# A hybrid attention and state-space step: 16-bit halves put together by VectorE, squares from SBUF, and two transposes moved from TensorE to the DMA

## The chip, the cores and the metric

The kernel runs on one NeuronCore of a Trainium2 chip. The core has TensorE (PE in the profile; its weight loads are PEld), VectorE (DVE), ScalarE (ACT), GpSimd (POOL) and SyncE (SP, which here only issues DMAs). Each works through its own queue of instructions in order, and semaphores tie them together. SBUF is the working memory of 128 partitions, PSUM the memory that TensorE writes to, in banks of 512 fp32 columns; 16 DMA engines move data. The metric is the device time of one execution in microseconds (us), as the median of several runs.

## The reference, cut to what matters

One layer is computed for 1024 prompt tokens and 8 samples of 16 tokens, 1152 tokens in all, model width 1024:

```python
h = rms_norm(x, norm_g) * (1 + scale) + shift            # scale, shift, gate from c @ w_ada
proj = h @ w_in                                          # q k v z_att z_ssd xbc dt gates
q, k = rms_norm(q, q_norm_g), rms_norm(k, k_norm_g)      # 16 heads of 64
o_att = attn(q, k, v)        # own chunk of 64 and 8 before it, relative bias; samples: 512 cached rows and own
att_branch = (o_att * silu(z_att)) @ w_att_proj
xbc, conv_new = causal_dwconv(xbc, ...)                  # width 4
xs, bm, cm = split(silu(xbc))                            # 32 heads of 64; 4 groups of 128 states
# per chunk, a_cs = cumsum(dt * a):
xdt = xs * dt
y = ((cm @ bm.T) * decay) @ xdt + (cm @ h) * exp(a_cs)
h = h * exp(a_cs[-1]) + bm.T @ (xdt * exp(a_cs[-1] - a_cs))
y = rms_norm((y + d_skip * xs) * silu(z_ssd), ssd_norm_g)
merged = sigmoid(g_att) * att_branch + sigmoid(g_ssd) * (y @ w_ssd_proj)
out = x + gate * (merged @ w_out)
```

Outputs are `out` for both groups, the new keys and values, the convolution's last rows and the final states.

## The kernel before

All matmuls of a projection ("dense") take fp32 operands as a high and a low part, so three matmuls stand for one product (L459, L460, L462). The 1152 tokens stand in the columns, in three groups of 384. A projection of 128 output rows is 72 such matmuls. Its weights are loaded to `raw` (L329, on SP, two places), split by ScalarE (L351, high part) and VectorE (L352, low part).

The stages, in order:

- **Start**, to about 85 us: adaLN and the norm give h.
- **Attention**, eight rounds u of two heads. `dense_gen` computes q, k, v with tokens in the rows (`dense_tok`, L523 to L525, 24 matmuls for each of nine token tiles into a PSUM bank of the pool `psd`, which has two). `ev` empties the bank: L948 copies q and k to SBUF (ScalarE), L950 squares them out of PSUM (ScalarE), L951 copies v (VectorE), L954 sums the squares. Then follows the dense projection of the gate z of the next round. `prelude` normalizes q and k on POOL and turns them by TensorE (L1001). `prompt` computes scores in rounds (L1166), softmax (L1053 bias and minimum, L1048 exponential, L1049, L1050), and `turn` transposes the probabilities by DMA. A DMA transpose takes 16-bit elements, so the 32-bit words are first taken apart into a plane of high halves and one of low halves (L1097, `planes`, ScalarE), each plane is transposed in blocks of 128x128 (L1098, on SP), and the halves are put together again (`words`): for head e = 0 by VectorE (L1106), for e = 1 by ScalarE (L1104). `weigh` (L1122) multiplies by v.
- `sample` does the same for the samples, in two groups of four per round: scores (L1221, L1224), softmax, then `transposed`, five TensorE transposes (L1060) and their copies out of PSUM (L1062 ScalarE, L1064 VectorE), the product with the cached v (L1248), a copy (L1254) and the turn back (L1258).
- **State-space**, about 770 to 1550 us, 16 pairs p of heads in four groups. `dense_gen` of a pair projects x and z (and a gate for ten of the pairs), `conv_gen` does the convolution (L1306 to L1316, result x with channels in the rows). `prelude` makes the decay matrices `me` (L1487 loads, L1499, L1503, L1505). `main` turns x by nine TensorE transposes (L1527), of which VectorE takes two scaled copies out of PSUM (L1531): `xw` for the state, `xd` for the output. Then come small splits (L1553, L1554), masks on POOL (L1561), chunk states (L1572, L1577, L1581), the output (L1599, L1606), what the earlier states give (L1619, L1624, L1625), the gating (L1632), and the samples' states (L1644, L1653).
- **Tail**, from about 1550 us: the remaining gates and the three last projections.

What sets the order: the code is written as generators. `run` drives the dense projection and, beside it, the lists `urgent` and `paced`; a planner's clock counts what a step costs TensorE (`yield n`) and how long others are expected to take (`pause`, `until`). The places for buffers are planned too: `walloc` waits until one is free, and a dense projection may be two pairs ahead at most (`AHEAD`). Then the tile framework's scheduler orders each engine's instructions; those in `late` keep their order.

Of the kernel before, what the change touches and what calls it, by code (L numbers as in the profile page):

```python
# [9 lines left out]
U16 = mybir.dt.uint16  # L10
AF = mybir.ActivationFunctionType
ALU = mybir.AluOpType

P = 128
# [8 lines left out]
HD = 64  # L23
# [10 lines left out]
BIG = -1e30  # L34

# [87 lines left out]
def trunk_kernel(ctx: ExitStack, tc: tile.TileContext, h):  # L123
# [41 lines left out]
    def pg(cols=512):  # L165
        return psg.tile([P, 512], F32, tag="g", name=nm("g"))[:, :cols]
# [663 lines left out]
    def until(t):  # L830
        while clock[0] < t:
            yield -1.0

    def pause(t):
        yield from until(clock[0] + t)
# [77 lines left out]

    sfree = [0.0]
# [14 lines left out]
    def attention(u):  # L929
# [4 lines left out]
        def dense_gen():  # L934
# [7 lines left out]
            def ev(t, ps):  # L942
# [7 lines left out]
                nc.scalar.activation(s.ap, ps[:, :2 * P], AF.Square)  # L950
# [104 lines left out]
        def transposed(p, pt, nt):  # L1055
            for j in range(0, nt, 4):
                n = min(4, nt - j)
                ps = pg()
                for s in range(n):
                    nc.tensor.transpose(ps[:, s * P:(s + 1) * P], p[:, (j + s) * P:(j + s + 1) * P], ident)  # L1060
                if j == 0:
                    nc.scalar.activation(pt[:, j * P:(j + n) * P], ps[:, :n * P], AF.Copy)  # L1062
                else:
                    nc.vector.tensor_copy(pt[:, j * P:(j + n) * P], ps[:, :n * P])  # L1064

        def prompt():
# [8 lines left out]

            def planes(x, at, n):
                return x.ap[:, at:at + n * P].bitcast(U16).rearrange("p (t k) -> p t k", t=2)

            def words(x, at, n):
                return x.ap[:, at:at + n * P].bitcast(U16).rearrange("p (k t) -> p t k", t=2)  # L1080

            def turn(m):
# [11 lines left out]
                for e in range(2):  # L1094
                    yield from until(probs[m] + 800 * e)
                    (x, at), (y, _) = place[m][e], turned[m][e]
                    nc.scalar.activation(planes(y, at, n), words(x, at, n), AF.Copy)  # L1097
                    dma(x.ap[:, at:at + n * P].bitcast(U16).rearrange("p (i k) -> p i k", k=P),  # L1098
                        y.ap[:, at:at + n * P].bitcast(U16), transpose=True)
                for e in range(2):  # L1100
                    yield from until(probs[m] + 800 * e + 7500)
                    (x, at), (y, _) = place[m][e], turned[m][e]
                    if e:
                        nc.scalar.activation(words(y, at, n), planes(x, at, n), AF.Copy)  # L1104
                    else:
                        nc.vector.tensor_copy(words(y, at, n), planes(x, at, n))  # L1106
# [4 lines left out]
                tpt[m] = clock[0] + 4500  # L1111
# [86 lines left out]
        def sample():  # L1198
# [6 lines left out]
            for bg in range(2):  # L1205
# [34 lines left out]
                transposed(p.ap, pt.ap, 5)  # L1240
                p.free()
                yield 550
                yield from pause(1800)
# [202 lines left out]
    def ssd(p):  # L1446
# [62 lines left out]
        def main():  # L1509
# [11 lines left out]
            for j in range(3):  # L1521
                n = min(4, 9 - 4 * j)
                c = slice(4 * j * P, (4 * j + n) * P)
                ps = pg()
                for s in range(n):
                    t0 = (4 * j + s) * P
                    nc.tensor.transpose(ps[:, s * P:(s + 1) * P], x.ap[:, t0:t0 + P], ident)  # L1527
                v4 = lambda t: t.rearrange("p (c e d) -> p c e d", e=2, d=HD)
                for dst, sc in ((xw, w4), (xd, d4)):
                    f = sc[:, 4 * j:4 * j + n, 2 * p:2 * p + 2].unsqueeze(3).to_broadcast([P, n, 2, HD])  # L1530
                    nc.vector.tensor_tensor(v4(dst.ap[:, c]), v4(ps[:, :n * P]), f, ALU.mult)  # L1531
                yield 107 * n
# [438 lines left out]
```

## Time and profile before

| | |
|---|---|
| median of three runs | 1965.84 us (1962.32 to 1969.33) |
| the profiled execution | 1968.7 us, span 1966.9 us |
| PE busy | 1910.4 us, 97% |
| DVE, ACT, POOL busy | 1171.7, 902.4, 326.3 us |
| mean granted TensorE clock | 0.995 |
| queue q1 (SP's DMAs) | 239.22 MB, 42.0% of 16 engines |

A row of the grouped lines reads: line, engine, operation, output<-inputs, shapes, count, then busy us and mean ns of one, then the engine's idle time before them and what ended it. A row of waits reads: engine, line, what it waited for, us in total, times, longest. A row by stretch gives each engine's busy time with its number of instructions, then the granted TensorE clock, the DMA engines' share and GB/s. L-numbers are lines of the kernel before. Busy time of a pipelined PE is not PE at its peak, so stretches without a gap are read together with their count of matmuls.

### The profile page before, as it was taken

How to read it: one execution, taken by the hardware profiler on the slowest of the kernel's cores; microseconds unless marked ns; L12 is line 12 of the kernel's file. 1: busy time of each engine (PE TensorE's matmuls, PEld its weight loads, DVE VectorE, ACT ScalarE, POOL GpSimd, SP SyncE). 2: the span in 40 equal slices, each digit the busy share in tenths (PEclk: the TensorE clock that was granted, in tenths of full speed). 3: DMA queues.
4: the chain of work that ended last, by engine and by line, in shares of the span. 5: the costliest groups of instructions: out<-in, count | busy, mean ns of one | idle time of the engine just before them, and what ended most of it. 6: DMA issues, size and time to landing. Idle time of an engine off the chain costs nothing.

```text
span 1966.9 us, 34369 instructions
## 1 busy us (share of the span) xinstructions
PE 1910.4 (97%) x13561; PEld 1814.8 (92%) x13561; DVE 1171.7 (60%) x2411; ACT 902.4 (46%) x1653; POOL 326.3 (17%) x624
## 2 busy tenths in 40 slices
PE   8999998999989999999999999999999999999999
PEld 5988887887878789999999999999999999999999
DVE  7456555555555675667666666675675333777732
ACT  8466657566666777344444443436342301111210
POOL 0312213121222201112312221122212200000000
PEclk9999999999999999999999999999999999999999
DMA  9155666556665565333433333323347642331241
GB/s 378 58 136 158 145 163 172 141 149 148 151 155 154 150 162 159 115 125 105 129 132 128 106 103 113 121 93 104 111 127 273 245 149 92 103 103 55 82 145 53
DMA packets 208184, 270.05 MB, mean 137 GB/s; under 512 B 141260, under 2 KB 142296, under 8 KB 208024
## 3 DMA queue, kind: packets, MB, share of 16 engines
q1 hardware_dynamic: 199064, 239.22, 42.0%
q0 software_dynamic: 8960, 28.65, 3.8%
q8 instruction: 107, 1.75, 0.4%
q14 instruction: 53, 0.43, 0.1%
HBM read 192.70 MB, written 43.66 MB: 120 GB/s over the span
## 4 chain that ended last, share of the span: by engine, by line
PE 78%; DMA 9%; ACT 6%; DVE 4%; issue 3%; SPq 1%; POOL 0%; ACTq 0%; DVEq 0%
PE d L459 13%; PE d L460 13%; PE d L462 13%; DMA arena<-arena 7%; PE s L459 6%; PE s L462 6%; PE s L460 6%; PE d L523 3%; PE d L524 2%; PE d L525 2%; ACT arena L1048 2%; ACT arena L1097 2%; PE g L1599 2%; PE g L1572 1%; PE g L1122 1%
## 5 line engine op out<-in xcount | busy, mean ns | idle before, releaser
L459 PE MATMUL d<-rarena 128*128 128x384 f32 x1528 | 521.2, 341 | 11.6 <-DVE arena L951 9.2
L462 PE MATMUL d<-rarena 128*128 128x384 f32 x1528 | 515.7, 338 | 1.3 <-DVE rarena L352 0.6
L460 PE MATMUL d<-rarena 128*128 128x384 f32 x1528 | 515.8, 338 | 0.0
L459 PEld LDWEIGHTS d<-rarena 128*128 128x128 f32 x1528 | 289.1, 189 | 17.4 <-issue 12.1
L460 PEld LDWEIGHTS d<-rarena 128*128 128x128 f32 x1528 | 288.9, 189 | 2.9 <-issue 2.8
L462 PEld LDWEIGHTS d<-rarena 128*128 128x128 f32 x1528 | 288.7, 189 | 2.5 <-DVE rarena L425 1.3
L351 ACT ACTIVATE rarena<-arena 128x1024 fp32r<-128x1024 f32 x91 | 96.4, 1059 | 318.7 <-PE s L460 228.1
L459 PE MATMUL s<-rarena 128*128 128x384 f32 x632 | 214.4, 339 | 0.0
L460 PE MATMUL s<-rarena 128*128 128x384 f32 x632 | 211.5, 335 | 0.0
L462 PE MATMUL s<-rarena 128*128 128x384 f32 x632 | 211.5, 335 | 0.0
L523 PE MATMUL d<-va_att,rarena 128*128 128x384 f32 (+1 forms) x559 | 195.5, 350 | 7.2 <-DVE arena L951 7.2
L525 PE MATMUL d<-va_att,rarena 128*128 128x384 f32 (+1 forms) x559 | 192.5, 344 | 0.0
L524 PE MATMUL d<-va_att,rarena 128*128 128x384 f32 (+1 forms) x559 | 192.0, 344 | 0.0
L352 DVE TENSOR_TENSOR rarena<-arena,rarena 128x1024 fp32r<-128x1024 f32 x91 | 111.7, 1227 | 75.6 <-ACT rarena L351 75.2
L1104 ACT ACTIVATE arena<-arena 128x1280 uint16<-128x1280 uint16 (+2 forms) x64 | 82.9, 1296 | 140.6 <-DMA arena<-arena 140.5
L1097 ACT ACTIVATE arena<-arena 128x1280 uint16<-128x1280 uint16 (+4 forms) x128 | 126.1, 998 | 18.1 <-DVE arena L1050 16.5
L523 PEld LDWEIGHTS d<-va_att,rarena 128*128 128x128 f32 x559 | 106.0, 190 | 17.1 <-DVE arena L951 9.4
L459 PEld LDWEIGHTS s<-rarena 128*128 128x128 f32 x632 | 118.8, 188 | 1.7 <-issue 1.6
L460 PEld LDWEIGHTS s<-rarena 128*128 128x128 f32 x632 | 118.8, 188 | 0.0
L462 PEld LDWEIGHTS s<-rarena 128*128 128x128 f32 x632 | 118.7, 188 | 0.0
L525 PEld LDWEIGHTS d<-va_att,rarena 128*128 128x128 f32 x559 | 106.4, 190 | 3.5 <-issue 3.3
L524 PEld LDWEIGHTS d<-va_att,rarena 128*128 128x128 f32 x559 | 106.4, 190 | 2.3 <-issue 1.8
(365 smaller groups left out, 3256.2 us busy)
## 6 DMA issues: line engine op xcount, KB each, us to landing
arena<-in_wall_dram SPq DMA_DIRECT2D x85, 512.0 KB, 3.7
arena<-in_kc_dram SPq DMA_DIRECT2D x64, 256.0 KB, 4.4
arena<-in_vc_dram SPq DMA_DIRECT2D x64, 256.0 KB, 3.7
arena<-acs_d SPq DMA_DIRECT2D x19, 576.0 KB, 3.8
gate_d<-arena POOLq DMA_DIRECT2D x48, 192.0 KB, 3.1
arena<-y_d SPq DMA_DIRECT2D x15, 576.0 KB, 4.8
arena<-in_wssd_dram SPq DMA_DIRECT2D x16, 512.0 KB, 3.3
arena<-eacs_d SPq DMA_DIRECT2D x28, 288.0 KB, 4.3
```

The source lines that it names most:

```text
L351: keep(nc.scalar.activation(hi.r[:, c], b.ap, AF.Copy))
L352: keep(nc.vector.tensor_tensor(lo.r[:, c], b.ap, hi.ap[:, c], ALU.subtract))
L459: nc.tensor.matmul(ps, hi.r[:, wc], kh.r[:, tok], start=k == 0, stop=False)
L460: nc.tensor.matmul(ps, hi.r[:, wc], kl.r[:, tok], start=False, stop=False)
L462: nc.tensor.matmul(ps, lo.r[:, wc], kh.r[:, tok], start=False, stop=k == nk - 1)
L523: nc.tensor.matmul(ps, kh.r[:, tok], wh, start=j == 0, stop=False)
L524: nc.tensor.matmul(ps, kh.r[:, tok], wl, start=False, stop=False)
L525: nc.tensor.matmul(ps, kl.r[:, tok], wh, start=False, stop=j == KT - 1)
L1048: nc.scalar.activation(p, p, AF.Exp, bias=sm_[:, 4 + e:5 + e], scale=-1.0, accum_out=sm_[:, 6 + e:7 + e])
L1097: nc.scalar.activation(planes(y, at, n), words(x, at, n), AF.Copy)
L1104: nc.scalar.activation(words(y, at, n), planes(x, at, n), AF.Copy)
L1599: nc.tensor.matmul(ps[he, s * P:(s + 1) * P], xd.ap[:, c * P + e * HD:c * P + e * HD + HD], me[e].ap[:, cs], start=True, stop=True)
```

## The change

Four edits:

1. `ev` squares the copy of q and k in SBUF instead of the PSUM bank.
2. `turn` puts the halves of both heads together on VectorE, with other planned times; the DMA is issued 900 ns of planned time after its copy.
3. `sample` takes the probabilities apart, transposes them by DMA and puts them together, in place of `transposed`.
4. `main` of the state-space stage does so with x (18 blocks of 128x128 halves), and makes `xd` and `xw` from the result in SBUF by two multiplies of 1152 columns.

```diff
+TURN = 9000
@@ attention, ev
                 nc.scalar.activation(c, ps[:, :2 * P], AF.Copy)
                 s = alloc(lay, "q", 2 * P)
-                nc.scalar.activation(s.ap, ps[:, :2 * P], AF.Square)
+                nc.scalar.activation(s.ap, c, AF.Square)
@@ turn
                 for e in range(2):
-                    yield from until(probs[m] + 800 * e)
+                    yield from until(probs[m] + 1000 * e)
                     (x, at), (y, _) = place[m][e], turned[m][e]
                     nc.scalar.activation(planes(y, at, n), words(x, at, n), AF.Copy)
+                    yield from until(probs[m] + 1000 * e + 900)
                     dma(x.ap[...], y.ap[...], transpose=True)
                 for e in range(2):
-                    yield from until(probs[m] + 800 * e + 7500)
+                    yield from until(probs[m] + 1000 * e + TURN)
                     (x, at), (y, _) = place[m][e], turned[m][e]
-                    if e:
-                        nc.scalar.activation(words(y, at, n), planes(x, at, n), AF.Copy)
-                    else:
-                        nc.vector.tensor_copy(words(y, at, n), planes(x, at, n))
+                    nc.vector.tensor_copy(words(y, at, n), planes(x, at, n))
...
-                tpt[m] = clock[0] + 4500
+                tpt[m] = clock[0] + 3500
@@ sample
                 yield from until(tp)
-                transposed(p.ap, pt.ap, 5)
+                nc.scalar.activation(planes(pt, 0, 5), words(p, 0, 5), AF.Copy)
+                dma(p.ap.bitcast(U16).rearrange("p (i k) -> p i k", k=P), pt.ap.bitcast(U16), transpose=True)
+                yield from pause(TURN)
+                nc.vector.tensor_copy(words(pt, 0, 5), planes(p, 0, 5))
                 p.free()
-                yield 550
-                yield from pause(1800)
+                yield from pause(3000)
@@ state-space, main
-            for j in range(3):
-                n = min(4, 9 - 4 * j)
...
-                for s in range(n):
-                    t0 = (4 * j + s) * P
-                    nc.tensor.transpose(ps[:, s * P:(s + 1) * P], x.ap[:, t0:t0 + P], ident)
...
-                for dst, sc in ((xw, w4), (xd, d4)):
...
-                    nc.vector.tensor_tensor(v4(dst.ap[:, c]), v4(ps[:, :n * P]), f, ALU.mult)
-                yield 107 * n
+            nc.scalar.activation(planes(xw, 0, 9), words(x, 0, 9), AF.Copy)
+            yield from pause(2500)
+            dma(xd.ap.bitcast(U16).rearrange("p (i k) -> p i k", k=P), xw.ap.bitcast(U16), transpose=True)
+            yield from pause(TURN + 1000)
+            nc.vector.tensor_copy(words(xw, 0, 9), planes(xd, 0, 9))
+            yield from pause(1800)
+            v4 = lambda t: t.rearrange("p (c e d) -> p c e d", e=2, d=HD)
+            for dst, sc in ((xd, d4), (xw, w4)):
+                f = sc[:, :, 2 * p:2 * p + 2].unsqueeze(3).to_broadcast([P, 9, 2, HD])
+                nc.vector.tensor_tensor(v4(dst.ap), v4(xw.ap), f, ALU.mult)
+                yield from pause(1300)
```

The planned times move work on every engine. Three places of the new order follow; line numbers of after are those of the changed kernel. In the rows, `d_` and `g_` are PSUM tiles, `arena`, `rarena` and `va_ssd` areas of SBUF.

ScalarE in the fourth attention round, before, at the emptying of two token tiles (L948 the copy, L950 the square, L1104 halves together, L1097 halves apart, L1048 exponentials):

```order
L1048 ACTIVATE arena<-arena 128x640 x2
L1097 ACTIVATE arena<-arena 128x1280
L1104 ACTIVATE arena<-arena 128x2x640
L1097 ACTIVATE arena<-arena 128x1280
L948 ACTIVATE arena<-d_2920 128x256
L950 ACTIVATE arena<-d_2920 128x256
L1048 ACTIVATE arena<-arena 128x640
L1104 ACTIVATE arena<-arena 128x2x640
L948 ACTIVATE arena<-d_2980 128x256
L950 ACTIVATE arena<-d_2980 128x256
```

The same place after (L957 the copy, L959 the square, L1089 halves apart, L1057 exponentials, L1230 the samples' halves apart):

```order
L1057 ACTIVATE arena<-arena 128x640 x2
L957 ACTIVATE arena<-d_2832 128x256
L959 ACTIVATE arena<-arena 128x256
L1089 ACTIVATE arena<-arena 128x1280 x2
L957 ACTIVATE arena<-d_2919 128x256
L1057 ACTIVATE arena<-arena 128x640
L959 ACTIVATE arena<-arena 128x256
L1230 ACTIVATE arena<-arena 128x1280
L957 ACTIVATE arena<-d_2979 128x256
L959 ACTIVATE arena<-arena 128x256
```

No putting together stands ahead of the copy any more, the square no longer reads a PSUM tile and can stand later, and the samples' taking apart has come in.

VectorE in the state-space stage, the second pair, before (L1531 the scaled copies out of PSUM, L1505 the decay matrix, L1554 a split, L352 weights, L1653 the samples' states of the pair before):

```order
L1531 TENSOR_TENSOR arena<-g_7994,arena 128x512 x2
L1531 TENSOR_TENSOR arena<-g_8001,arena 128x512 x2
L1653 TENSOR_TENSOR qa_ssd<-qa_ssd,g_7951 128x512
L1531 TENSOR_TENSOR arena<-g_8017,arena 128x128 x2
L1505 TENSOR_TENSOR arena<-arena 128x1152
L1554 TENSOR_TENSOR rarena<-arena,rarena 64x128 x2
```

The same after (L1518 halves together, L1523 the two multiplies, L1497 the decay matrix, L1616 and L1617 the output of the pair before, L1624 its gating, L354 weights, L1546 the split):

```order
L1518 COPY va_ssd<-va_ssd 128x2x1152
L1497 TENSOR_TENSOR arena<-arena 128x1152
L1616 TENSOR_TENSOR arena<-arena,g_7802 128x512
L1523 TENSOR_TENSOR va_ssd<-va_ssd,arena 128x1152
L1617 TENSOR_TENSOR arena<-arena 128x512
L1523 TENSOR_TENSOR va_ssd<-va_ssd,arena 128x1152
L1624 SCALAR_TENSOR_TENSOR arena<-arena,va_ssd 128x1152
L354 TENSOR_TENSOR rarena<-arena,rarena 128x1024
L1546 TENSOR_TENSOR rarena<-va_ssd,rarena 64x128
```

Six multiplies out of PSUM have become one copy and two multiplies in SBUF, and they stand among the output sums of the pair before.

SP in the state-space stage after, around the transposes of two pairs (L1516 the transpose, L1479 and L1483 loads of the decay's sums, L1485 the samples' states, L331 weights, L1272 the convolution's rows; before, the same queue has only such loads):

```order
L1479 DMA arena<-acs_d 128x1152
L1516 DMA_TRANSPOSE arena<-va_ssd 128x18x128
L1483 DMA va_ssd<-eacs_d 64x1152 x2
L331 DMA arena<-in_wall_dram 128x1024
L1479 DMA arena<-acs_d 128x1152
L331 DMA arena<-in_wall_dram 128x1024
L1485 DMA qa_ssd<-in_h_dram 128x1024
L1272 DMA arena<-in_sconv_dram 128x24
L331 DMA arena<-in_wall_dram 128x1024 x2
L1479 DMA arena<-acs_d 128x1152 x2
L1516 DMA_TRANSPOSE va_ssd<-arena 128x18x128
```

The transpose waits for ScalarE's copy, and what is behind it on SP waits with it.

On TensorE, the new order has these numbers of dense matmuls between the last L1619 of one pair and the first L1572 of the next, for the fifteen gaps: 213, 210, 93, 201, 213, 108, 156, 201, 213, 108, 93, 200, 183, 112, 225.

More of the change, by code (lines that the diff above doesn't have):

```diff
@@ L911, in rsqrt_dram, with planes, words @@
         yield from pause(2300)
+    def planes(x, at, n):
+        return x.ap[:, at:at + n * P].bitcast(U16).rearrange("p (t k) -> p t k", t=2)
+    def words(x, at, n):
+        return x.ap[:, at:at + n * P].bitcast(U16).rearrange("p (k t) -> p t k", t=2)
     sfree = [0.0]
@@ L1074, in prompt @@
             pairs = {0: 3, 1: 2, 2: 1, 3: 0}
[L1076 to L1080, printed above, removed]
             def turn(m):
```

14 lines of the change are left out of this document (removed).

## The prediction

> **What bounds the kernel now.** I read the page's first block, then the busy time by stretch, then PE's own waits, the stretches at half clock, and a timeline around one stall.
>
> ```profile
> span 1966.9 us, 34369 instructions
> PE 1910.4 (97%) x13561; PEld 1814.8 (92%) x13561; DVE 1171.7 (60%) x2411; ACT 902.4 (46%) x1653; POOL 326.3 (17%) x624
> ...
> core 0: us, PE busy (x) PEld busy (x) DVE busy (x) ACT busy (x) POOL busy (x), PEclk, DMA share, GB/s
> 250.00:415.00 165.00, 153.42 (x1232) 136.37 (x1231) 90.96 (x277) 105.03 (x193) 36.84 (x74) 0.98 0.62 155
> ...
> 900.00:1100.00 200.00, 200.00 (x1427) 197.56 (x1426) 130.98 (x214) 93.83 (x194) 43.72 (x79) 1.00 0.38 124
> 1100.00:1300.00 200.00, 199.93 (x1424) 196.88 (x1423) 132.31 (x213) 79.05 (x154) 42.86 (x78) 1.00 0.33 106
> ...
> 1640.00:1967.00 327.00, 323.12 (x1865) 322.80 (x1863) 194.07 (x299) 53.24 (x48) 0.00 (x0) 1.00 0.29 94
> ```
>
> TensorE sets the time. In the state-space stage (900 to 1300) it has no gap, at full clock (the third number from the right); there a matmul that goes is time that goes, as long as what replaces it comes in time. In the attention stage (250 to 415, two of its eight rounds) it stands idle 11.6 of 165 us. The tail, dense matmuls alone, gives a price for later: 323.12 us by 1865 is 0.173 us a matmul. Who ends PE's gaps:
>
> ```profile
> PE d L459 <- DVE arena L951: 9.2, 5, 2.1
> ...
> PE s L1221 <- DVE arena L1053: 7.2, 6, 1.4
> PE d L523 <- DVE arena L951: 7.2, 6, 1.7
> PE g L1258 <- ACT arena L1254: 5.1, 4, 1.7
> PE g L1122 <- ACT arena L1104: 3.3, 3, 1.9
> ...
> PE g L1060 <- DVE arena L1050: 1.9, 2, 1.5
> ```
>
> Columns: us in total, times, longest. The largest sum is 16.4 us, of two places that wait for L951, VectorE's copy of v out of PSUM, the last reader of a token tile's bank. And after some of these waits PE goes at half clock; the first and the last of six such stretches, all in the attention stage:
>
> ```profile
> 171.20:174.40 3.20, 3.20 (x12) 3.20 (x12) 1.77 (x3) 1.88 (x4) 2.47 (x10) 0.50 0.99 266
> ...
> 731.00:734.20 3.20, 3.20 (x14) 2.76 (x17) 2.40 (x8) 1.41 (x5) 0.00 (x0) 0.50 1.02 201
> ```
>
> The granted clock there is 0.50: of each stretch of 3.2 us half is lost, 1.6 us, and 9.6 in the six. One stall, in order of time:
>
> ```profile
> 392.46 1.65 ACT L1104 ACTIVATE arena<-arena 128x1280 uint16<-128x1280 uint16 x1
> ...
> 393.97 1.24 ACT L1097 ACTIVATE arena<-arena 128x1280 uint16<-128x1280 uint16 x1
> ...
> 395.12 0.36 ACT L948 ACTIVATE arena<-d 128x256 f32<-128x256 f32 x1
> 395.38 0.37 ACT L950 ACTIVATE arena<-d 128x256 f32<-128x256 f32 x1
> ...
> 395.78 0.29 DVE L951 COPY arena<-d 128x128 f32<-128x128 f32 x1 [3.39 <-ACT arena L950]
> ...
> 396.13 0.50 PE L523 MATMUL d<-va_att,rarena 128*128 128x384 f32 x1 [1.63 <-DVE arena L951]
> ```
>
> ScalarE puts halves together (L1104), takes the next apart (L1097), and only then empties the bank (L948, the square L950); VectorE's copy waits for L950, and PE for that.
>
> **The change part by part.** Prices of what goes and what comes:
>
> ```profile
> 860.54 0.98 PE g L1527 x9
> ...
> 401.62 0.55 PE g L1060 x5
> ...
> L1104 ACT ACTIVATE arena<-arena 128x1280 uint16<-128x1280 uint16 x32 | 53.1, 1659 | 53.3 <-DMA arena<-arena 53.3
> L1097 ACT ACTIVATE arena<-arena 128x1280 uint16<-128x1280 uint16 x64 | 80.4, 1264 | 11.4 <-DVE arena L1050 11.2
> L1106 DVE COPY arena<-arena 128x1280 uint16<-128x1280 uint16 x32 | 29.7, 928 | 41.7 <-DMA arena<-arena 41.7
> L1531 DVE TENSOR_TENSOR arena<-g,arena 128x512 f32<-128x512 f32 x50 | 31.4, 681 | 7.9 <-PE g L1527 7.9
> L1531 DVE TENSOR_TENSOR arena<-g,arena 128x128 f32<-128x128 f32 x25 | 6.1, 278 | 0.0
> L1505 DVE TENSOR_TENSOR arena<-arena,va_ssd 128x1152 f32<-128x1152 f32 x11 | 14.8, 1354 | 18.6 <-ACT arena L1503 18.6
> ...
> DMA to landing us min/median/max: 2.7/3.0/6.1
> ```
>
> *Transposes leave PE.* x: 16 pairs by 0.98 us, 15.7 us, in a stage without a gap. Samples: 16 groups by 0.55, 8.8. Together 24.5. PE does nothing in their place.
>
> *The bank is free one ScalarE instruction earlier.* The square (0.37 us) now reads the copy in SBUF, so L951 follows L948. And L1104 (1.66 us, one in two of the putting-together copies) leaves ScalarE's queue for VectorE's, where it is 0.93. At five of the six L523 stalls L1104 stands ahead of L948 as in the timeline above, and 1.66 and 0.37 are more than the longest of them, 1.7. I take these five, 5.5 of the 7.2 (the sixth, 1.7, has no L1104 ahead). At the five L459 stalls it is L1097 and L1002 that stand ahead; 0.37 of about 1.8 is sure, the rest depends on the new order, so half: 4.6 (bounds 1.9 and 9.2).
>
> *The order moves.* L1258, which turns the samples' result back, had in four rounds only scores ahead of it; now 21 to 40 dense matmuls, 3.6 us or more, stand between its input's matmuls and it, and the longest of these waits is 1.7: 5.1 us go. L1060's wait goes with L1060: 1.9. Of six stretches at half clock I let three go with their stalls: 4.8 (bounds 0 and 9.6).
>
> So far: 15.7 + 8.8 + 5.5 + 4.6 + 5.1 + 1.9 + 4.8 = 46.4 us.
>
> *What x's new way costs.* Before: 0.98 on PE, then six multiplies out of PSUM, 4 x 0.681 + 2 x 0.278 = 3.3: 4.3 us. Now in a row: the halves apart on ScalarE, 2304 elements, 1.264 x 1.8 = 2.3; the DMA; the halves together on VectorE, 0.928 x 1.8 = 1.7; two multiplies of 1152 at 1.354, 2.7. No row has a transpose of 18 blocks; the DMA's bounds are 3.0 (the median of those of 2 to 10 blocks) and 11.0 (the longest, 6.1, by 18/10). I take 4.5, near the median, since most of the 128 land there whatever their size. Sum 11.2 us, bounds 9.7 and 17.7. It starts where the pair before frees its places (about its last L1619) and must end at L1572. In the new order 93 to 225 dense matmuls stand between the two, in five of the fifteen gaps only 93 to 112: 16 to 19 us. That covers 11.2, with queues it may not:
>
> ```profile
> ACT rarena L351 <- PE s L460: 228.1, 54, 12.8
> ...
> SPq L329 <- DVE rarena L352: 494.4, 71, 20.0
> ```
>
> ScalarE stands 4.2 us on average behind a weight copy that waits for PE, and SP 7.0 us behind a weight load that waits for VectorE; x's copy and x's DMA are queued behind these. One of each on top of 11.2 is 22.4, 3 to 6 us over the five tight gaps, and not every pair meets them. I take 2 us in five gaps: 10 (bounds 0 and 57, the latter below). The other ten gaps, 27 us and more, cover it. What is late next behind x is L1553 and the mask on POOL, then L1644, with 45 to 85 matmuls ahead.
>
> *DVE.* A pair: out 3.3, in 1.7 + 2.7, 1.1 more; a round of attention: some 6 us of halves and 1.3 of the samples more, on 45 busy of 82. No bound, but a queue for L951. *SP:* 32 transposes more, 16 of 18 blocks (128x128 of 16 bits) and 16 of 10; the attention stage's transposes are issued 0.9 us after their copy, so SP waits less in front of them. *The samples' way* (copy 1.26, DMA 3.0, halves 0.93 against L1060's 0.55 and copies) has over 30 token matmuls, 5 us, ahead of L1248, planned with 12 us. For VectorE's longer queue and these later operands I take 0.5 us in 16 groups: 8 (bounds 0 and 16).
>
> *The tail:* the last pair frees its places some 31 us later (117 dense matmuls of cover against 297), still ten us ahead of the first projection; 0, bound 5.
>
> **The sum.** 46.4 less 18 is 28.4. The profiled execution took 1968.7 us (1966.9 of span); 1940.3 is what it would take. It stands 2.9 us above the median of 1965.84, so the median I forecast is 1937.
>
> A rule of the Trainium skill speaks against the change: "VectorE: DVE Perf Modes", section "The three transpose paths", has 390 ns for a 128x128 bf16 block on TensorE and 1309 by DMA, and its rules give TensorE the preference where PSUM may be the target. By that 18 blocks would be 23.6 us (an estimate from the page), and x's way 30.3 instead of 11.2. This trace agrees for TensorE's side in kind, but transposes of 2 to 10 blocks land in 3.0 us here, none after 6.1, where ten would be 13. For 18 no run here shows it; what a late landing would do is the first rival.
>
> **Rivals.** *Late x: slower.* The place is L1572 of each pair. If landing grows to 11.0 us and each x meets one ScalarE and one SP wait, its way is 17.7 + 4.2 + 7.0 = 28.9, over the five tight gaps by 10 to 13 us, some 57 in all: 1968.7 - 46.4 + 8 + 57 - 2.9 = 1984. It decides where the waits come to more than 38 us, 8 in each tight gap. For it: SP's and ScalarE's waits above, and a dense order that runs up to two pairs ahead only. Against it: the 3.0 us, and transposes that were waited for by PE only 3.3 us in the whole run. By the page's figure a transpose would end 12.6 us later still in each tight gap, and the time would be near 2047, an estimate that no row here bears out.
>
> *Attention keeps its stalls.* The waits on L951 and the half clock come back behind VectorE's longer queue. Only PE's 24.5 and the state-space cost of 10 count: 1968.7 - 14.5 - 2.9 = 1951. For it: five stalls of which 0.37 us alone is sure to go.
>
> *Nothing to measure.* Those stalls stay, and new ones of 8 us in the attention stage and 16 in the other take what PE saved: 1968.7 - 24.5 + 24 - 2.9 = 1965. Against it: the state-space stage's gaps are wide in ten of fifteen.
>
> **How the numbers follow.** Forecast 0.60, own range 1918 to 1948 (28.4 saved, with the bounds of the half clock, of L459's stalls and of the samples each way); attention keeps its stalls 0.18; nothing to measure 0.08 (within 0.3%, 6 us, about what a measurement of this kernel can tell from no change); late x 0.14. The first two are faster: 0.78. The range for 8 in 10 runs from 1916 (the other 4.8 of half clock and 4.6 of L459's stalls gone too, and 7 of new waits in place of 18) to 1967, past the second and the third case; left out is most of late x, and a little below.
>
> **What would show it.** Right: L1527 and L1060's groups gone and PE busy near 1880; the copy of v waiting for the copy of q and k, PE's waits on it under 8 us; PE still 99% busy from 900 to 1300; fewer than six stretches at 0.50. Wrong: PE waits at L1572 or L1599 for VectorE over 10 us in sum, x's transpose landing over 8 us, SP waiting on ScalarE ahead of it, a stretch at 0.50 after 770.

## The result and the profile after

The changed kernel takes 1920.33 us (median of 4 runs, 1920.08 to 1923.85), the kernel before 1965.82 (4 runs, 1962.32 to 1969.33): a ratio of 0.977, 95% interval 0.975 to 0.979. The profiled execution took 1920.13 us, its span 1918.1. The head of its page:

```profile
span 1918.1 us, 33842 instructions
PE 1871.8 (98%) x13337; PEld 1783.8 (93%) x13337; DVE 1246.6 (65%) x2427; ACT 884.5 (46%) x1605; POOL 353.7 (18%) x624
```

Busy time by stretch, cut at the same places of the program: from 84 us to the last token matmul of the attention stage, and from there to the tail's first matmul. First before, then after (second number: the length; third: PE's busy time):

```profile
84.00:663.70 579.70, 542.85 (x4337) 484.51 (x4336) 320.36 (x977) 368.67 (x685) 132.97 (x260) 0.99 0.61 153
663.70:1608.80 945.10, 938.66 (x6697) 915.26 (x6700) 599.75 (x1041) 422.23 (x823) 186.24 (x348) 1.00 0.42 135
```

```profile
84.00:622.30 538.30, 521.77 (x4265) 469.54 (x4264) 368.73 (x1030) 328.77 (x630) 146.33 (x260) 0.99 0.69 171
622.30:1559.40 937.10, 920.34 (x6542) 897.92 (x6540) 625.95 (x1005) 443.24 (x829) 200.32 (x348) 1.00 0.49 148
```

The attention stage is 41.4 us shorter, the state-space stage 8.0; what follows, the tail, is 0.6 longer (358.7). In the attention stage PE's gaps (length less busy) fell from 36.9 to 16.5 us, in the other they grew from 6.4 to 16.8. Who ends the gaps after (L461 and L525 are the first of three dense and of three token matmuls, L960 the copy of v, L1462 an eviction of z on VectorE, L1246 and L1250 the old L1254 and L1258):

```profile
PE d L461 <- DVE arena L960: 11.1, 6, 2.7
PE d L461 <- DVE arena L1462: 8.6, 2, 7.8
...
PE g L1250 <- ACT arena L1246: 4.7, 2, 3.5
...
PE d L525 <- DVE arena L960: 0.5, 1, 0.5
```

And a wait that stands on no PE row. First before: what ScalarE waited for ahead of putting halves together (L1104). Then after: ScalarE ahead of the copy of q and k (L957, the old L948), and VectorE ahead of putting together (L1096):

```profile
ACT arena L1104 <- DMA arena<-arena: 140.5, 46, 9.0
```

```profile
ACT arena L957 <- PE d L527: 37.3, 22, 6.8
...
DVE arena L1096 <- DMA arena<-arena: 83.7, 65, 4.2
```

Before, ScalarE stood 140.5 us in front of transposes that had not landed, with the copies of q and k queued behind. After, none of this is left on ScalarE, and L957 waits for PE alone: it is ready when the bank is full.

The one long gap of the state-space stage, in order of time on three engines (L1516 x's transpose, L1518 its halves together, L1523 the first multiply; between L1518 and L1523 stand the samples' states and the decay matrix, behind them weights, each 1.2 to 1.4 us):

```profile
1405.51 1.95 SPq L1516 DMA_TRANSPOSE va_ssd<-arena  x1
...
1409.46 1.46 DVE L1518 COPY arena<-va_ssd 128x2304 uint16<-128x2304 uint16 x1 [2.03 <-DMA va_ssd<-arena]
...
1413.35 1.35 DVE L1523 TENSOR_TENSOR va_ssd<-arena 128x1152 f32<-128x1152 f32 x1
...
1415.75 0.55 DVE L1462 SCALAR_TENSOR_TENSOR arena<-arena,d 128x384 f32<-128x384 f32 x1
...
1416.35 0.69 PE L461 MATMUL d<-rarena 128*128 128x384 f32 x1 [7.83 <-DVE arena L1462]
```

PE does not wait for x. It waits for a bank, and the eviction that frees it is queued on VectorE behind x's halves, which wait for the DMA. That wait is 2.03 of the 7.83 us; the five instructions from 1409.46 to 1415.75 take most of the rest, and ScalarE's part of the eviction (L1461) came only at 1411.07. Half clock goes with the stall (a stretch of after; the granted clock is third from the right):

```profile
1413.20:1420.10 6.90, 3.75 (x12) 3.75 (x13) 6.63 (x9) 0.24 (x1) 0.00 (x0) 0.51 0.60 194
```

After has this one and two of 3.4 us at 396 and 550 us; before had six of the short kind, five of them in the attention stage.

### The profile page after: what moved, and what is told of

It reads as the page before. It is cut to its first block, busy times and chain, and to the rows that moved or that the text cites. A ratio compares the mean times of both kernels' runs of the same rounds, so it can differ in the third digit from the quotient of the medians.

```text
span 1918.1 us, 33842 instructions
## 1 busy us (share of the span) xinstructions
PE 1871.8 (98%) x13337; PEld 1783.8 (93%) x13337; DVE 1246.6 (65%) x2427; ACT 884.5 (46%) x1605; POOL 353.7 (18%) x624
## 4 chain that ended last, share of the span: by engine, by line
PE 81%; DMA 8%; DVE 6%; ACT 3%; issue 2%; SPq 0%; POOL 0%; DVEq 0%; ACTq 0%; POOLq 0%
PE d L461 13%; PE d L462 13%; PE d L464 13%; DMA arena<-arena 6%; PE s L461 6%; PE s L464 6%; PE s L462 6%; PE d L525 4%; PE d L526 3%; PE d L527 3%; PE g L1591 2%; PE g L1112 2%; PE g L1564 1%; PE g L1611 1%; PE g L462 1%
## 5 line engine op out<-in xcount | busy, mean ns | idle before, releaser
L461 PE MATMUL d<-rarena 128*128 128x384 f32 x1528 | 522.9, 342 | 20.4 <-DVE arena L960 11.1
L461 PEld LDWEIGHTS d<-rarena 128*128 128x128 f32 x1528 | 288.8, 189 | 26.8 <-DVE arena L960 13.1
L461 PE MATMUL s<-rarena 128*128 128x384 f32 x632 | 214.2, 339 | 0.0
L525 PE MATMUL d<-va_att,rarena 128*128 128x384 f32 (+1 forms) x559 | 197.4, 354 | 0.5 <-DVE arena L960 0.5
L354 DVE TENSOR_TENSOR rarena<-arena,rarena 128x1024 fp32r<-128x1024 f32 x91 | 112.8, 1239 | 66.4 <-ACT rarena L353 66.3
L1057 ACT ACTIVATE arena<-arena 128x640 f32<-128x640 f32 (+2 forms) x144 | 101.2, 704 | 114.1 <-DVE arena L1174 52.2
L1096 DVE COPY arena<-arena 128x1280 uint16<-128x1280 uint16 (+4 forms) x128 | 92.2, 720 | 84.5 <-DMA arena<-arena 83.7
L1089 ACT ACTIVATE arena<-arena 128x1280 uint16<-128x1280 uint16 (+4 forms) x128 | 125.9, 1000 | 30.4 <-DVE arena L1059 25.0
L461 PEld LDWEIGHTS s<-rarena 128*128 128x128 f32 x632 | 118.8, 188 | 3.0 <-issue 2.9
L525 PEld LDWEIGHTS d<-va_att,rarena 128*128 128x128 f32 x559 | 105.3, 188 | 14.4 <-issue 13.1
L526 PEld LDWEIGHTS d<-va_att,rarena 128*128 128x128 f32 x559 | 105.4, 189 | 0.7 <-DVE arena L662 0.4
```

The lines of the kernel that those rows point to most:

```text
L354: keep(nc.vector.tensor_tensor(lo.r[:, c], b.ap, hi.ap[:, c], ALU.subtract))
L461: nc.tensor.matmul(ps, hi.r[:, wc], kh.r[:, tok], start=k == 0, stop=False)
L525: nc.tensor.matmul(ps, kh.r[:, tok], wh, start=j == 0, stop=False)
L526: nc.tensor.matmul(ps, kh.r[:, tok], wl, start=False, stop=False)
L1057: nc.scalar.activation(p, p, AF.Exp, bias=sm_[:, 4 + e:5 + e], scale=-1.0, accum_out=sm_[:, 6 + e:7 + e])
```

## The experiments

Each was timed against the kernel before on the same chip; pairs of numbers are medians, ratios carry 95% intervals.

### Each part alone

**x by DMA**: the diff's last part added to the kernel before, and nothing else.

> The kernel before with x of each pair turned by DMA, nothing else changed; the order moves from the last round of attention on. Theory one (PE's 15.7 us come off whole, and what is lost again is one or two accidents of the order, like the single 7.8 us stall at 1416 us of the changed kernel and the half clock behind it): 8 to 16 us less than before, waits of PE in the state-space stage few and long. Rival (x comes late in every tight gap, about 2 us in each, as the prediction's term of 10 us has it): about 6 us less, and waits at the products of x in five or more pairs. The attention stage as before in both.

1956.02 against 1965.23 us, ratio 0.996 (0.994 to 0.997). From 755 us to the tail one wait is left, at 1451 us; the changed kernel has one of the same kind at 1416:

```profile
PE d L461 <- DVE arena L1473: 6.7, 1, 6.7
```

Theory one: 9.2 us, with one accident and not one in every tight gap.

**The square from SBUF**:

```diff
-                nc.scalar.activation(s.ap, ps[:, :2 * P], AF.Square)
+                nc.scalar.activation(s.ap, c, AF.Square)
```

> The kernel before with the square read from the copy in SBUF, nothing else changed; the order stays but for a few rows. Theory one (the copy of v waits for the last reader of the bank, so each of the 11 waits of PE on it becomes one square, 0.37 us, shorter): 4 us less, up to 7 if stretches at half clock go with them. Rival (what stands in ScalarE's queue ahead sets these waits, and VectorE has other work at that point): within 1 us of before.

1963.3 against 1965.23, ratio 0.9986 (0.9974 to 0.9997). The waits on v's copy fell from 16.4 to 9.9 us, but others took their place (L1069 is the old L1060, L1125 the old L1122, which had 1.9 and 3.3):

```profile
PE d L461 <- DVE arena L960: 9.9, 6, 1.7
PE g L1069 <- DVE arena L1059: 9.1, 6, 2.2
...
PE g L1125 <- ACT arena L1107: 8.5, 10, 1.5
```

About 2 us, between the two theories; the interval, from 0.6 to 5 us, excludes neither the 4 of theory one nor the 1 of the rival.

**The samples by DMA**:

```diff
-                transposed(p.ap, pt.ap, 5)
+                nc.scalar.activation(planes(pt, 0, 5), words(p, 0, 5), AF.Copy)
+                dma(p..., pt..., transpose=True)
+                yield from pause(TURN)
+                nc.vector.tensor_copy(words(pt, 0, 5), planes(p, 0, 5))
```

> The kernel before with the samples' probabilities turned by DMA, nothing else changed; the order of the whole attention stage moves. Theory one (PE's 8.8 us and the 1.9 us of waits in front of them go, the new operands come in time): about 11 us less. Rival one (new waits of 0.5 us in each of 16 groups): 3 us less. Rival two (much of the attention stage's gain of 41 us lies here, since the evictions of these transposes on ScalarE and VectorE stood ahead of others): 20 us or more less, with the waits of the scores for VectorE and of the dense matmuls for the copy of v shrinking too.

1979.28 against 1965.23, ratio 1.007 (1.005 to 1.009): 14 us slower, which none of the theories had. PE saves its transposes, the samples' scores no longer wait, and PE waits elsewhere (L1010 turns q and k, after L990, POOL's scaling of them):

```profile
PE g L1010 <- POOL arena L990: 16.0, 5, 4.2
PE d L461 <- DVE arena L960: 15.1, 7, 4.1
PE g L1252 <- ACT arena L1248: 9.2, 5, 4.3
```

In this order L1010 stands right behind L1252 in five of the rounds, with no dense matmul between. A round's plan repeats, so one bad place counts five times or more.

**The halves by VectorE, and later**: the `turn` part of the diff alone.

> The kernel before with the halves put together by VectorE alone and at the later planned times, nothing else changed. Theory one (five of six waits of the token matmuls on the copy of v go with the copy that ScalarE no longer has in its queue; little else): 5 to 10 us less. Rival (the later times let the plan put dense matmuls where scores waited for VectorE, and most of the attention stage's gain of 41 us is here): 20 us or more less, with the waits of the score matmuls (7.2 us before) gone.

1953.33 against 1965.23, ratio 0.994 (0.992 to 0.996): 12 us. The token matmuls' waits went (7.2 to 0.7), those of the samples' scores (L1222, the old L1221, 7.2) stayed, and those of the dense matmuls grew from 9.2:

```profile
PE d L461 <- DVE arena L960: 13.9, 6, 3.5
PE s L1222 <- DVE arena L1062: 6.9, 7, 2.6
```

A little above theory one's 5 to 10; the rival is wrong in its place, since the scores still wait.

The four parts alone sum to 9 us, the whole is 45. Much of the difference is half clock, as the mean granted clocks of all runs show. The missing share of the clock times the span is an estimate of what half clock costs at most: by medians some 6 us in the kernel before, 9 with x alone, 6 with the square, 24 with the samples (their clocks are 0.984 to 0.990, those of the kernel before 0.993 to 1.000), 12 with the halves, and 9 in the changed kernel. Without it the parts alone come to some 35 us and the whole to 48, so about 13 us are left to parts acting together. The clocks are given to three places, so each figure is good to about 1 us.

### One part left out of the change

**Without the halves** (`turn` as before, the rest changed):

> The changed kernel with the halves put together as before (one of two on ScalarE, earlier planned times); square, samples and x as in the changed kernel. The parts done alone gave 9, 2, 12 us less and, for the samples, 14 us more, together 9 less where the whole gives 45. Theory one (the samples' new way and the halves' new times make one order between them: without the halves the order stays near that of the samples alone): about 1968, near the 1979 of the samples alone less the 9 of x and the 2 of the square, with PE's waits for POOL's scaled q and k (16 us there) still in it. Rival (the samples' loss came from the bank's release, which the square mends): 1945 or less.

1958.32 against 1966.82, ratio 0.995 (0.993 to 0.997). The waits on POOL are gone, the scores wait for nothing, but these stand:

```profile
PE d L461 <- DVE arena L960: 21.6, 11, 4.0
PE g L1252 <- ACT arena L1248: 12.2, 5, 4.3
```

Between the two theories, nearer the first: beside the other parts the halves are worth some 37 us (by the medians), alone 12.

**Without the samples** (`transposed` on TensorE again, the rest changed):

> The changed kernel with the samples' probabilities turned by TensorE as before; square, halves and x as in the changed kernel. Theory one (its order in the attention stage is nearly that of the halves alone): about 1942, the 1953 of the halves alone less 9 and 2, so that the samples are worth 22 us beside the halves though they cost 14 without them. Rival (the samples are worth PE's 10.7 us wherever they stand, and the loss alone was an accident of one order): about 1931.

1953.82 against 1966.82, ratio 0.993 (0.990 to 0.996): 12 us above the figure of theory one. The samples cost 14 us alone and save some 32 beside the halves. Not all of that is theirs: of the 26.4 us between the two profiled executions only 18 arise before the last token matmul, and the state-space stage, which this edit does not touch, has 13.4 us of waits on the eviction of z where the changed kernel has 8.6. The scores wait again, as in every kernel that turns the samples on TensorE (6.9 to 11.2 us); in those that don't, at most 1.6 us of these waits are left:

```profile
PE s L1222 <- DVE arena L1062: 11.2, 7, 4.1
```

So these waits go with the samples' part.

### Engine and planned times apart

**VectorE alone, at the old times**, on the kernel before:

```diff
-                    if e:
-                        nc.scalar.activation(words(y, at, n), planes(x, at, n), AF.Copy)
-                    else:
-                        nc.vector.tensor_copy(words(y, at, n), planes(x, at, n))
+                    nc.vector.tensor_copy(words(y, at, n), planes(x, at, n))
```

> The kernel before with all halves put together by VectorE, at the planned times of before, nothing else changed; TensorE's order stays but for a few rows. Theory one (what matters is that ScalarE's queue loses the 1.66 us copy ahead of the copy of q and k): the waits of the token matmuls on the copy of v (7.2 us before) go, 4 to 8 us less, a good part of the 12 of the halves alone. Rival (the planned times are what brought it: later halves let the plan lay other work between): within 3 us of before, since the copy now stands in VectorE's queue, ahead of the copy of v.

1976.98 against 1965.15, ratio 1.006 (1.005 to 1.008): 12 us slower. PE's waits, then one case in order of time (L963 sums the squares, L986 is the first of POOL's steps up to L990):

```profile
PE g L1010 <- POOL arena L990: 16.1, 5, 3.3
...
PE g L1010 <- DVE arena L1171: 9.2, 7, 1.9
...
PE d L461 <- DVE arena L960: 2.7, 1, 2.7
```

```profile
239.88 0.38 ACT L959 ACTIVATE arena<-d 128x256 f32<-128x256 f32 x1
...
240.84 0.90 DVE L1106 COPY arena<-arena 128x1280 uint16<-128x1280 uint16 x1 [3.68 <-DMA arena<-arena]
...
245.59 0.29 DVE L960 COPY arena<-d 128x128 f32<-128x128 f32 x1
245.80 0.41 DVE L963 TENSOR_REDUCE arena<-arena 128x4 f32<-128x256 f32 x1
...
246.30 0.20 POOL L986 TENSOR_SCALAR arena<-arena 128x16 f32<-128x16 f32 x1 [27.02 <-DVE arena L963]
...
254.06 0.48 PE L1010 MATMUL g<-arena 128*128 128x128 f32 x1 [3.20 <-POOL arena L990]
```

The waits on v's copy do go (16.4 to 2.7). But VectorE now stands in front of the transposes, and L960 and L963 come 5.3 us after ScalarE has finished with the bank; POOL starts late, and PE waits at L1010, 25.3 us in all. The wait has changed its engine, and some 11 of the 12 us are half clock by the same estimate (mean clocks of 0.990 and 0.991). With the later times as well (halves alone), L1010's waits are 3.7 us, and the kernel is some 24 us faster than this one.

**One of two on ScalarE again, at the new times**, in the changed kernel: the same edit backwards.

> The changed kernel with one of two of the copies that put halves together back on ScalarE, at the planned times of the changed kernel; TensorE's order all but unchanged. Theory one (the engine alone, at the old times, cost 12 us more, so the gain is the times' and the order's, and VectorE's queue is the tighter one): within 5 us of the changed kernel, perhaps less than it. Rival (ScalarE's copy of q and k behind the 1.66 us copy is what made the token matmuls wait, and it would again): 8 us more or above, with 5 us or more of waits on the copy of v added to the 11 of the changed kernel.

1942.28 against 1962.9, ratio 0.989 (0.987 to 0.992): 22 us slower than the changed kernel. One wait (L1097 is L1104's copy):

```profile
327.75 1.62 ACT L1097 ACTIVATE arena<-arena 128x1280 uint16<-128x1280 uint16 x1
329.24 0.36 ACT L957 ACTIVATE arena<-d 128x256 f32<-128x256 f32 x1
...
329.62 0.29 DVE L960 COPY arena<-d 128x128 f32<-128x128 f32 x1 [0.43 <-ACT arena L957]
...
329.97 0.44 PE L461 MATMUL d<-rarena 128*128 128x384 f32 x1 [2.35 <-DVE arena L960]
```

ScalarE's waits in front of L1097, and two of PE's (L1253 is the old L1258):

```profile
ACT arena L1097 <- DMA arena<-arena: 79.0, 43, 4.6
```

```profile
PE d L461 <- DVE arena L960: 12.8, 5, 4.4
...
PE g L1253 <- ACT arena L1249: 8.6, 6, 2.0
...
PE g L1010 <- DVE arena L1164: 5.7, 4, 2.8
```

The rival in size, and its queue is right. But the copy of v has only 1.7 us more of the waits; the turns of the samples' result and of q and k have 9.4 more, and four more short stretches at half clock some 7 (by the mean clocks of all runs about 6). So the engine is worth 22 us in the new order and costs 12 in the old one.

### x's cover

**x issued earlier**, in the changed kernel:

```diff
-            yield from pause(2500)
+            yield from pause(600)
             dma(xd..., xw..., transpose=True)
-            yield from pause(TURN + 1000)
+            yield from pause(TURN)
```

> The changed kernel with x's DMA planned 600 ns instead of 2500 behind its copy and the halves 9000 instead of 10000 behind that, so that SP issues it ahead of other loads. Theory one (the one long stall of the state-space stage, 7.8 us at 1416 with half clock for 6.8 us, comes of x's transpose late on SP and the evictions behind it in VectorE's queue): 5 to 11 us less than the changed kernel, no stall over 2 us in that stage. Rival (that place has too much on VectorE whatever x does): the stall stays, within 3 us.

1920.68 against 1966.82, ratio 0.977 (0.974 to 0.980): the changed kernel's. The stall stays, 7.7 us. The planned time was not what held x back, as SP's wait in this run shows (L1617 sums the output of the pair before; the place that x is transposed into comes free behind it):

```profile
SPq L1516 <- DVE arena L1617: 3.4, 1, 3.4
```

**x turned twice**, in the changed kernel: the `dma(xd..., xw..., transpose=True)` line written twice.

> The changed kernel with x's DMA transpose issued twice into the same place, so that x of each pair is some 5 us later and SP is held some 3 us longer; the plan and the orders are as in the changed kernel. Theory one (16 to 19 us of dense matmuls cover x's 11.3 us in the tight gaps, and the one stall at 1416 us is a late start): 3 to 10 us more than the changed kernel, nearly all of it in that stall and the half clock behind it. Rival (x's way is at the edge of its cover in all five tight gaps, as the prediction's first rival has it): 15 us more or above, with new waits at the products of x or at the dense matmuls in four or more pairs.

1936.91 against 1965.15, ratio 0.986 (0.984 to 0.988): some 17 us more than the changed kernel. The waits from 755 to 1560 us, in the changed kernel nearly all one stall, are now at six places (L1637 the samples' states, L1592 the old L1599, L1565 the old L1572):

```profile
PE d L461 <- DVE arena L1462: 10.3, 3, 6.1
PE g L1637 <- POOL rarena L1554: 2.7, 2, 1.6
PE g L1592 <- DVE arena L1574: 2.3, 1, 2.3
...
PE g L1565 <- DVE va_ssd L1524: 1.9, 1, 1.9
```

The rival is nearer: x's way is near the edge of its cover in several pairs. Its places are another matter: most of the waits are evictions and steps behind x, one is the products of x.

### Two that go further

**v by ScalarE**, in the changed kernel:

```diff
                 nc.scalar.activation(c, ps[:, :2 * P], AF.Copy)
+                nc.scalar.activation(v.ap[:, t * P:(t + 1) * P], ps[:, 2 * P:NQ], AF.Copy)
                 s = alloc(lay, "q", 2 * P)
                 nc.scalar.activation(s.ap, c, AF.Square)
-                nc.vector.tensor_copy(v.ap[:, t * P:(t + 1) * P], ps[:, 2 * P:NQ])
```

> The changed kernel with v copied out of the bank by ScalarE, right behind q and k, instead of VectorE; order of TensorE all but unchanged. Theory one (the six waits of 11.1 us on this copy that are left come from what stands ahead in VectorE's queue): 5 to 10 us less than the changed kernel, PE's waits on ScalarE at most 4 us in their place. Rival (ScalarE's own queue sets them: its copy of q and k comes late as well): within 3 us of the changed kernel, the waits now booked on ScalarE.

1912.44 against 1966.82, ratio 0.972 (0.970 to 0.975): 8 us by the medians below the changed kernel (whose ratio's interval begins at 0.9752, where this one ends at 0.9749). The 11.6 us of waits on v's copy are gone, and 0.7 on ScalarE is what came:

```profile
PE d L461 <- DVE arena L1462: 9.3, 1, 9.3
...
PE d L461 <- ACT arena L959: 0.7, 1, 0.7
```

With one engine to empty the bank, VectorE's queue no longer holds it.

**The last z first**: in addition, for the last pair but one, x's halves are put together behind the evictions of the last z; `late` makes the scheduler keep that order.

```diff
+            if p == NPAIR - 2:
+                yield from ready(lambda: p + 1 in zdone)   # z of the last pair is done
-            nc.vector.tensor_copy(words(xw, 0, 9), planes(xd, 0, 9))
+            late(nc.vector.tensor_copy(words(xw, 0, 9), planes(xd, 0, 9)))   # that pair alone
```

> The changed kernel with v copied by ScalarE and, for the last pair but one alone, x's halves put together behind the evictions of the last z on VectorE instead of ahead of them. Theory one (in that place the evictions stood behind x, which waited for its DMA, and the bank's release was held by VectorE's order): the stall of 9.3 us at 1410 shrinks to 4 or less and the half clock behind it with it, 4 to 9 us less than the 1912 of v by ScalarE alone. Rival (x of that pair then comes late for its own products, and the wait only moves): within 3 us of 1912, with a new wait at the products of x.

1909.56 against 1965.15, ratio 0.972 (0.970 to 0.974), the lowest median of all. The stall shrank from 9.3 to 6.3 us, less than theory one has; its eviction (L1464) still stands behind other work on VectorE:

```profile
PE d L461 <- DVE arena L1464: 6.3, 1, 6.3
```

The 3 us against the version without it are within the intervals. It is faster than the changed kernel by some 10 us.

## Why the prediction was right, and where it was not

The forecast was 1937 us with a range of 1916 to 1967, and its own case ran from 1918 to 1948; 1920.33 lies in both, near the low end. Added up from the bounds that it names, its own case would run from 1920 to 1953. Its low end needed all the half clock and all of L459's waits to go; neither went, and the time came out there in another way, which is luck. The sum had 28.4 us; by the spans it is 48.8. Nearly all the difference is in the attention stage: 22.7 by the terms (8.8 + 5.5 + 4.6 + 5.1 + 1.9 + 4.8 less 8), 41.4 measured.

- *Transposes leave PE* (24.5): right. Counted from matmul to matmul, L1527 took 14.3 us and L1060 9.7.
- *L523's waits on v* (5.5 of 7.2): right in size, 6.7 went. The mechanism (L1104 ahead of the bank's emptying) is not shown by that: these waits went as well with the square alone (none left) and with the samples alone (0.7), where one of two copies stays on ScalarE. With the ScalarE half back in the new order one such case is there, but only 1.7 us in sum; in the old order VectorE alone only moved the wait.
- *L459's waits* (4.6): wrong. They went from 9.2 to 11.1. The step left "the rest" to the new order; there L960 stands behind other work of VectorE (at 394.9 us behind L1059, L354 and L1014, 0.55, 1.22 and 0.74 us). That v copied by ScalarE removes them shows which queue it was.
- *L1258* (5.1): wrong, 0.4 went. The dense matmuls ahead of it did not always cover it: 4.7 us are left in two waits, one of 3.5.
- *L1060's wait* (1.9): right; 1.5 of it lay in this stage.
- *Half clock* (4.8 for three of six stretches): right in the attention stage of the two profiled executions, where five became two; in the state-space stage the one of 3.2 us became one of 6.9. Over all runs the term is not borne out: the mean clock was 0.993 to 1.000 before (43 runs, median 0.997) and 0.994 to 0.996 after, so half clock cost some 3 us more by the estimate above, and not less.
- *Not in the sum:* the waits of the samples' scores (L1221, 7.2 to 0.2), which go with the samples' part, those of L1122 (3.3), L1166 (1.7) and L1001 (1.6 to 0.2), and some 7 us inside PE's busy time: counted from matmul to matmul, the stage's 800 of L1122 took 51.4 us before and 47.7 after, its 504 of L1166 48.9 and 45.9. Why is open. Together 20; the errors of the other steps nearly cancel, which is luck, so this is what the forecast missed in that stage.
- *New waits in attention* (8, bounds 0 and 16): 0. VectorE's 48 us more of work in that stage show at PE only in L459's 1.9.
- *The state-space cost* (10 us, 2 in each of five tight gaps): right in size, wrong in place. Gaps grew by 10.3 us, 7.8 of them one stall at a dense matmul. The pieces of x's way add up to 11.3 us, the forecast had 11.2: 2.12 apart, 4.9 to land (the row of the transposes below, of four recorded landings), 1.50 together, two times 1.35 to 1.43. End to end, from the start of the copy to the end of the second multiply, it took 11.7 to 27.4 us, about 16 in the middle; in five pairs SP issued the transpose 2.5 to 11.0 us after the copy. The forecast's queue was real, and the dense matmuls covered most of it.

```profile
DMA to landing us min/median/max: 3.9/4.9/6.9
```

The step that failed is the list of attention's stalls. It priced L1104 by its 1.66 us, and only where it stood ahead of L948 at a wait of a token matmul. The row quoted for that price carried "53.3 <-DMA" at its end, and the prediction read only the duration: ScalarE stood 140.5 us in 46 waits in front of L1104, up to 9.0 at a time. With half of these copies back on ScalarE, 79.0 us of such waits and 22 us of time come back, and only 1.7 of them show at the copy of v; the rest is spread over what else ScalarE feeds. Nor did the list see that the samples' part takes the scores' 7.2 us with it. And it charged 8 us for new waits behind a longer VectorE queue, which at PE came to 1.9 in this order, though the kernel with VectorE alone was 12 us slower in the old one.

Of the rivals, late x was real but small: it needed 38 us more in its gaps, and 17 us is what x cost with a second transpose. That attention keeps its stalls was half right: L459's stayed (11.1 us), L523's went. That there is nothing to measure was wrong. The rule of the Trainium skill, "VectorE: DVE Perf Modes", section "The three transpose paths", which would make 18 blocks 23.6 us (the prediction's estimate from the page), does not agree with this case: 4.9 us is the median of the four landings recorded, and all sixteen of x's halves began at most 7.3 us after the issue. (The 3.0 us that the prediction took for most of the 128 transposes before is the median of the 8 that the trace records.) Of the signs, PE's busy time (1871.8 for 1880), the copy of v behind that of q and k, and fewer half-clock stretches came; PE stayed busy from 900 to 1300 us (199.23 of the first 200, 200.00 of the second).

PE's waits on v's copy came to 11.6 us and not under 8, and the stretch at 0.50 after 770 us, named as a sign of being wrong, is there at 1413.

What stays open: why the planned times and the samples' way, each harmful or small in the old order, make a good order together. The runs show which waits go with which edits, and that much of the harm is half clock behind the longer ones; which row of the plan decides was not tried.

## What to carry to other kernels

Read the idle time in front of an instruction as well as its duration: a cheap copy that waits for a DMA, on an in-order queue that also empties PSUM, can cost much more than its own time (here 22 us, with 79.0 us of such waits). Give a bank's emptying to one engine (worth some 8 us here), and keep that engine's queue free of waits for transfers. Where a planner sets the order, the parts of a change are not additive (9 us apart, 45 together), so test a part by leaving it out as well as by doing it alone, and look at the mean clock before you call the rest an interaction.

## What the runs showed of the hardware

In this case a DMA transpose takes little longer for more blocks of 128x128. Few landings are recorded (four of the sixteen of x with 18 blocks, 3.9 to 6.9 us, and two of the samples' sixteen with 10 blocks, 4.6 and 5.3), so I also read when the copies began that waited for one: x's halves 3.9 to 7.3 us after the issue (14 cases, 5.6 in the middle), the samples' 3.2 to 6.0 (15 cases, 4.7 in the middle). That is about 1 us more for almost twice the blocks. The waiting copies behind the prompt's transposes of 10 blocks began 3.0 to 7.1 us after the issue (25 cases, 4.9).

Half clock goes by where a stall falls and not by its length alone. In every trace the stretches at 0.50 start a whole number of cells of 3.413 us apart, the one in which the execution ends included, and the others last one to four cells. In the changed kernel a stall of 2.66 us, ended at 548.58, lies for the most part in one cell, and the next cell is at 0.50. The kernel with the square alone has a wait of 3.10 us, ended at 746.76, which two cells share; its mean clock is 1.000, though its attention stage has more gaps than that of the kernel before (42.0 us to 36.9). The cell of the changed kernel, then the two of the square alone (second number: the length; third: PE's busy time):

```profile
546.29:549.70 3.41, 1.12 (x6) 1.12 (x7) 3.41 (x8) 1.88 (x4) 0.11 (x1) 1.00 0.99 311
```

```profile
742.12:745.53 3.41, 1.54 (x9) 1.22 (x8) 1.42 (x3) 2.43 (x6) 0.00 (x0) 1.00 0.21 49
745.53:748.95 3.42, 2.19 (x11) 1.98 (x12) 2.25 (x6) 3.42 (x6) 0.00 (x0) 1.00 0.42 134
```

PE is idle 2.29 us in the first, 1.87 and 1.23 in the others. Over the fourteen traces, from 60 us on, all 66 cells at full clock with 1.9 us or more of idle time are followed by one at 0.50, 11 of the 63 with 1.5 to 1.9, and none of the 7478 with less. The cells lie differently against the start of each execution, so the same stall can cost its clock in one and not in another. What decides between 1.5 and 1.9 us, and why a stretch lasts one cell or four, is open. The Trainium skill, "TensorE: Matmul & The Clock Gate", section "Why this matters for your kernels", advises against idle gaps over about 3 us; in this case shorter ones lost the clock and one of 3.1 did not.
